# An encoder layer on one core: w_ga's weight units split by two DMAs from d = 2 on

## The chip, the cores and the metric

The kernel runs on one core of a Trainium2 chip. The metric is the device time of one execution in microseconds (us). A core has five engines that run their own instruction streams: PE (matrix products), DVE and ACT (elementwise work), POOL (elementwise work, and the issue of DMAs) and SP (here only the issue of DMAs). They wait for each other through semaphores, and each works strictly in the order of its stream. DMAs are issued on two queues here, SP's and POOL's; sixteen DMA engines carry out both.

## The reference

One layer of a bidirectional encoder, with 1024 positions and a model width of 1024, all in 32-bit floats. The part that the change touches is the merge of two branches:

```python
z = h @ w_in
u, v, q, k, va, gate_a, gate_b = jnp.split(z, cuts, axis=-1)
a_out = gmlp_branch(u, v, gm_v_g, gm_w_s, gm_b_s) @ w_a
b_out = window_attention_branch(q, k, va, q_norm_g, k_norm_g, attn_sink) @ w_b
merged = jax.nn.sigmoid(gate_a) * a_out + jax.nn.sigmoid(gate_b) * b_out
x = x + gt1 * (merged @ w_o)
```

`h` is the normalised and modulated input. A feed-forward sub-layer follows, which the change does not touch. The columns of `w_in` that give `gate_a` are called w_ga in the kernel, those for `gate_b` w_gb; w_a and w_b lie side by side in w_ab.

## The kernel before

**Products in three parts.** PE works on a 32-bit format with a shortened mantissa (`F32R`). To keep the accuracy, every operand is split into a high part, its value rounded to that format, and a low part, the rest. A product is then three: high by high, high by low, low by high, in this order (`mm3`, line 154).

**Units.** Weights come in units of 128 x 1024 values, 512 KB. `unit` (line 146) loads one over SP's queue into a tile called `raw`, lets ACT copy it into a tile `wh` (the copy rounds), and lets DVE subtract the two into a tile `wl`. The pool `wpool` has three buffers each for `raw`, `wh` and `wl`, so each new unit has to wait until the unit that holds its buffer is used up.

**Stages.** `half` (line 513) runs twice, each time over 512 of the positions: q, k and v, then attention mixed with the u products and the gates of d = 0 and 1, then a loop over d (line 868), then a loop for w_o (line 919). The feed-forward part follows. In the loop over d, tile d makes 128 of the 1024 output channels of `merged`, transposed. From d = 2 on it needs three units: w_gb[d], w_ab[d], w_ga[d]. PE's order in a tile is the w_gb gate (8 steps of 3 products of 128 x 128 by 128 x 512), the w_b product (4 steps of 3), the w_ga gate (8 steps of 3), the w_a product (4 steps of 3). ACT turns each gate's sum into a tanh, DVE multiplies it with the branch's product and adds the two, and the result is split for the w_o loop. Each tile also handles two (first half) or three (second half) units of w_ada2, which DVE reduces from `raw` tiles (`ada_next`, line 503); the first half loads a block of x as well.

**The order of the work.** From d = 2 on nothing fixes the order by hand: a scheduler orders each engine's stream, hands out the buffers and sets the waits. The units of the next tile are split while PE works on the present one. DMAs of SP's queue keep the order in which the program issues them (`load`, line 126). POOL issues the stores of x1 in the w_o loops and DMAs of the feed-forward part, and in the loop over d nothing from d = 2 on.

Of the kernel before, what the change touches and what calls it, by code (L numbers as in the profile page):

```python
# [8 lines left out]
F32 = mybir.dt.float32  # L9
F32R = mybir.dt.float32r  # L10
BF16 = mybir.dt.bfloat16
AF = mybir.ActivationFunctionType
ALU = mybir.AluOpType
# [3 lines left out]
P = 128  # L17
# [16 lines left out]
UNIT = 1024  # L34
# [4 lines left out]
def kernel(  # L39
# [22 lines left out]
    nc = tc.nc  # L62
# [19 lines left out]
    V, A, G, T = (Engine(e) for e in (nc.vector, nc.scalar, nc.gpsimd, nc.tensor))  # L82
# [4 lines left out]
    wpool = ctx.enter_context(pool("wpool", 3))  # L87
# [9 lines left out]
    def nm(s):  # L97
        n_names[0] += 1
        return f"{s}_{n_names[0]}"

    def mm_bank():
        return psum.tile([P, 512], F32, tag="mm", name=nm("mm"))
# [7 lines left out]
    def stream(tag):  # L110
        return t2.tile([P, 512], F32, tag=tag, name=nm(tag), bufs=2)

    def midt(dt, shape):
        return mid.tile([P, 2048], dt, tag="mid", name=nm("mid")).rearrange(
            "p (a b) -> p a b", a=shape
        )
# [9 lines left out]
    def load(dst, src):  # L126
        tc.keep_in_program_order(nc.sync.dma_start(dst, src))
# [13 lines left out]
    def raw_unit(src):  # L141
        r = wpool.tile([P, UNIT], F32, tag="raw", name=nm("raw"))
        load(r, src)
        return r

    def unit(src, eng=None, raw=None):
        r = raw if raw is not None else raw_unit(src)
        h = wpool.tile([P, UNIT], F32R, tag="wh", name=nm("wh"))
        l = wpool.tile([P, UNIT], F32R, tag="wl", name=nm("wl"))
        A.copy(h, r)  # L150
        (eng or V).tensor_tensor(l, r, h.bitcast(F32), op=ALU.subtract)
        return h, l

    def mm3(out, a, b, first, last):
        T.matmul(out, a[0], b[0], start=first, stop=False)
        T.matmul(out, a[0], b[1], start=False, stop=False)
        T.matmul(out, a[1], b[0], start=False, stop=last)
# [130 lines left out]
    def ss_tile():  # L288
        return small.tile([P, 640], F32, tag="ss", name=nm("ss"), bufs=1)
# [3 lines left out]
    def sumsq(src, first, ss):  # L293
        if first:
            A.activation(ss, src, AF.Square)
        else:
            q = tmp()
            A.activation(q, src, AF.Square)
            V.tensor_tensor(ss, ss, q, op=ALU.add)
# [10 lines left out]
    def split(src, dh, dl, eng=None):  # L310
        A.copy(dh, src)
        (eng or V).tensor_tensor(dl, src, dh.bitcast(F32), op=ALU.subtract)
# [190 lines left out]
    def ada_next(n):  # L503
        for _ in range(n):
            if ada_queue:
                col, gain = ada_queue.pop(0)
                ada_dot(raw_unit(w_ada2[col - GT1]), col)
                ada_end(col, gain)

    def x_rows(hf, k):  # L510
        return xT[k * P : (k + 1) * P, hf * HALF : (hf + 1) * HALF]

    def half(hf):
# [4 lines left out]
        if hf == 0:  # L518
# [33 lines left out]
            ada_dot(r[:, 1, :], SH1)  # L552
            V.reciprocal(rcol[0], root)
            wq = unit(None, V, wq0)
            wk = [wpool.tile([P, UNIT], F32R, tag=x, name=nm(x)) for x in ("wh", "wl")]
            A.copy(wk[0], wk0)
# [19 lines left out]
        for k in range(KT):  # L576
# [25 lines left out]
            if k == 4:  # L602
                wk = unit(w_kv[1], V)
            if k % 2 == 1 and k < KT - 1:
                wq_next = unit(w_q[(k + 1) // 2], V)
# [80 lines left out]
        def gate(wg):  # L686
            pg = mm_bank()
            gate_part(wg, pg, range(KT))
            return pg
# [161 lines left out]
        def gate_act(pg):  # L851
            sg = tmp()
            A.activation(sg, pg, AF.Tanh, scale=0.5)
            return sg
# [13 lines left out]
        for d in range(KT):  # L868
            if d % 4 == 0:
                mH[d // 4] = midt(F32R, 4)  # L870
                mL[d // 4] = midt(F32R, 4)
            ms = []
            in_order[0] = d < 2
            if d > 1:
                wg2 = unit(w_gb[d])
                wab = unit(w_ab[d])
                wg1 = unit(w_ga[d])
            else:
                wg1 = wg2 = None
                wab = units[9 + d]  # L880
            for (wg, o, br) in ((wg2, 512, (oH, oL)), (wg1, 0, (gH, gL))):
                sg = gate_act(gate(wg)) if d > 1 else sgs.pop(0)
                pb = mm_bank()
                for k in range(4):
                    kc = slice(o + k * P, o + (k + 1) * P)
                    mm3(pb, (wab[0][:, kc], wab[1][:, kc]),
                        (br[0][:, k, :], br[1][:, k, :]), k == 0, k == 3)
                V.scalar_tensor_tensor(out=sg, in0=sg, scalar=1.0, in1=pb, op0=ALU.add, op1=ALU.mult)
                ms.append(sg)
            V.tensor_tensor(ms[0], ms[0], ms[1], op=ALU.add)  # L890
            split(ms[0], mH[d // 4][:, d % 4, :], mL[d // 4][:, d % 4, :])
            in_order[0] = False
            if d > 1:
                ada_next(2 + hf)
            if hf == 0:
                xk = stream("hs")
                load(xk, x_rows(1, d))
                if d == 0:
                    ssn = ss_tile()[:, :HALF]
                in_order[0] = d == 0  # L900
                sumsq(xk, d == 0, ssn)
                in_order[0] = False
# [54 lines left out]
        sums.append(ss)  # L957

    half(0)
    half(1)  # L960


# [559 lines left out]
```

## Time and profile before

| what | value |
|---|---|
| time, median of 2 runs | 1256.95 us (1256.83 to 1257.07) |
| span of the profiled execution, first to last instruction | 1255.1 us |
| DMA packets | 67773, 214.25 MB |
| SP's queue | 155.59 MB |
| POOL's queue | 57.68 MB |
| read from HBM over the span | 170.24 MB |
| w_ga's loads | 16 of 512 KB on SP's queue, 4.0 us from issue to landing (median) |

The times are of the timed runs; the profile is of one execution, and its span leaves out what lies before the first and after the last instruction. In the profile's rows L75 is the line of a helper through which all engine calls go, so groups are told apart by the names of the tiles: out<-in, with shape, type, count, then busy time, the mean of one in ns, and the idle time of the engine before them with what ended it. PEld is the loading of weights into PE, which overlaps with the products. A row of the timeline has start and length in us, engine, line, operation and tiles. A row of the DMA issues has the queue, the count, the size and the median time in us from issue to landing.

### The profile page before, as it was taken

The page shows a single profiled execution, that of the slowest core. Times are in us where ns is not written, and L with a number is a line of the kernel's source. Part 1 is how long each engine was busy: PE and PEld are TensorE (multiplying, and loading weights), DVE is VectorE, ACT ScalarE, POOL GpSimd, SP SyncE. Part 2 cuts the span into 40 slices and gives each one's busy share as a digit, 9 for nine tenths or more (in the row PEclk, how much of TensorE's full clock was granted, in tenths as well). Part 3 has the DMA queues.
Part 4 walks back from the last instruction along what each step waited for, and adds up shares of the span by engine and source line. Part 5 has one row for each costly group of instructions (what it writes and reads, how often), then busy time and mean ns, then how long its engine had stood idle before and what let it go on. Part 6 is the DMA issues. An engine that isn't in the chain of part 4 may idle for free.

```text
span 1255.1 us, 15405 instructions
## 1 busy us (share of the span) xinstructions
PE 1234.1 (98%) x5714; PEld 1025.1 (82%) x5714; DVE 861.5 (69%) x1404; ACT 543.5 (43%) x867; POOL 132.7 (11%) x148
## 2 busy tenths in 40 slices
PE   5999999999999999999999999999999999999998
PEld 4888888888888888888888888888888887888887
DVE  8998875557468786666698766666666666455646
ACT  5467853334257772334454333333333334433342
POOL 0123310000032330000100000001010000010001
PEclk9999999999999999999999999999999999999999
DMA  9422145546522126665712454464554449896652
GB/s 362 169 84 67 52 143 184 177 159 211 197 70 67 51 89 196 201 194 209 250 36 102 147 189 151 154 213 182 205 189 180 168 168 357 280 328 187 196 161 101
DMA packets 67773, 214.25 MB, mean 171 GB/s; under 512 B 7793, under 2 KB 7793, under 8 KB 62450
## 3 DMA queue, kind: packets, MB, share of 16 engines
q1 hardware_dynamic: 56450, 155.59, 37.5%
q0 software_dynamic: 11248, 57.68, 12.7%
q8 instruction: 45, 0.74, 0.2%
q14 instruction: 30, 0.25, 0.1%
HBM read 170.24 MB, written 42.99 MB: 170 GB/s over the span
## 4 chain that ended last, share of the span: by engine, by line
PE 86%; DVE 6%; ACT 3%; DMA 3%; issue 1%; SPq 0%; POOL 0%; ACTq 0%; DVEq 0%
PE mm L75 47%; PE at L75 39%; DVE mid L75 2%; DVE wl L75 2%; ACT wh L75 1%; DMA mid<-in_w_ada_dram 1%; DMA hs<-in_xT_dram 1%; ACT lb L75 1%; DVE xs L75 0%; DMA mid<-in_xT_dram 0%; ACT mid L75 0%; DVE ws L75 0%; DMA raw<-in_w_o_dram 0%; DVE hid L75 0%; DMA raw<-in_w_q_dram 0%
## 5 line engine op out<-in xcount | busy, mean ns | idle before, releaser
L75 DVE TENSOR_TENSOR wl<-raw,wh 128x1024 fp32r<-128x1024 f32 x147 | 180.7, 1231 | 122.9 <-ACT wh L75 121.5
L75 ACT CAST wh<-raw 128x1024 fp32r<-128x1024 f32 x161 | 168.9, 1053 | 218.7 <-PE mm L75 126.7
L75 PE MATMUL mm<-mid,wh 128*128 128x512 f32 x736 | 227.8, 390 | 0.8 <-DVE mid L75 0.6
L75 PE MATMUL mm<-h,wh 128*128 128x512 f32 x608 | 187.9, 390 | 0.0
L75 PEld LDWEIGHTS mm<-mid,wh 128*128 128x128 f32 x736 | 137.7, 188 | 30.3 <-DVE mid L75 1.0
L75 PE MATMUL mm<-mid,wl 128*128 128x512 f32 x368 | 143.2, 389 | 0.0
L75 PEld LDWEIGHTS mm<-h,wh 128*128 128x128 f32 x608 | 113.7, 188 | 23.4
L75 PE MATMUL mm<-wh,h 128*128 128x512 f32 x384 | 129.7, 399 | 2.4 <-ACT h L75 2.3
L75 PE MATMUL mm<-h,wl 128*128 128x512 f32 x304 | 118.3, 389 | 0.0
L75 DVE TENSOR_TENSOR wl<-ws,wh 128x1024 fp32r<-128x1024 f32 (+1 forms) x55 | 62.0, 1128 | 43.6 <-ACT wh L75 43.6
L75 PEld LDWEIGHTS mm<-wh,h 128*128 128x128 f32 x384 | 71.7, 189 | 17.3 <-ACT h L75 3.2
L75 PEld LDWEIGHTS mm<-mid,wl 128*128 128x128 f32 x368 | 69.1, 188 | 14.4
L75 ACT CAST wh<-ws 128x1024 fp32r<-128x1024 f32 (+1 forms) x55 | 53.6, 974 | 58.6 <-DVE ws L75 42.1
L75 PE MATMUL mm<-wl,h 128*128 128x512 f32 x192 | 75.9, 395 | 0.0
L75 PE MATMUL at<-h,wh 128*128 128x512 f32 x240 | 74.1, 390 | 0.0
L75 PEld LDWEIGHTS mm<-h,wl 128*128 128x128 f32 x304 | 57.1, 188 | 12.0
L75 DVE SCALAR_TENSOR_TENSOR raw<-raw,silu_c 128x1024 f32<-128x1024 f32 x32 | 39.1, 1222 | 34.4 <-DMA raw<-in_w_ada_dram 33.5
L75 DVE TENSOR_TENSOR ol<-raw,oh 128x1024 fp32r<-128x1024 f32 x30 | 36.7, 1224 | 31.6 <-ACT oh L75 29.8
L75 ACT ACTIVATE xs<-xs 128x512 f32<-128x512 f32 x21 | 13.3, 633 | 96.4 <-DVE xs L75 96.4
L75 PE MATMUL at<-wl,wh 128*128 128x512 f32 x136 | 53.0, 390 | 0.7 <-DVE wl L75 0.7
L75 PE MATMUL at<-wh 128*128 128x512 f32 x136 | 53.0, 390 | 0.4 <-DVE mid L75 0.4
L75 PE MATMUL at<-wh,wl 128*128 128x512 f32 x136 | 52.9, 389 | 0.0
(244 smaller groups left out, 2459.8 us busy)
## 6 DMA issues: line engine op xcount, KB each, us to landing
raw<-in_w_ada_dram SPq DMA_DIRECT2D x32, 512.0 KB, 3.5
raw<-in_w_gate_dram SPq DMA_DIRECT2D x28, 512.0 KB, 4.1
tA<-hid POOLq DMA_DIRECT2D x11, 1024.0 KB, 5.0
tB<-hid POOLq DMA_DIRECT2D x11, 1024.0 KB, 4.9
wo<-in_w_out_dram POOLq DMA_DIRECT2D x22, 512.0 KB, 6.3
wS<-wo POOLq DMA_DIRECT2D x11, 1024.0 KB, 5.2
raw<-wS SPq DMA_DIRECT2D x44, 256.0 KB, 3.7
raw<-tB SPq DMA_DIRECT2D x44, 256.0 KB, 4.6
```

What stands on the lines that cost most here:

```text
L75: ins = f(*args, **kw)
```

## The change

From d = 2 on the units of w_ga are made by a new function. The high part is loaded straight from HBM into `wh` by a DMA on POOL's queue whose target type is `F32R`, so that it converts. ACT writes the negated high part into `wl`. A second DMA on POOL's queue then reads the same weights again and adds them onto what `wl` holds. No `raw` tile is used, and DVE has no part in it. w_gb's and w_ab's units, and w_ga's first two, are made as before.

```diff
+    def unit_by_dma(src):
+        h = wpool.tile([P, UNIT], F32R, tag="wh", name=nm("wh"))
+        l = wpool.tile([P, UNIT], F32R, tag="wl", name=nm("wl"))
+        nc.gpsimd.dma_start(h, src)
+        A.mul(l, h.bitcast(F32), -1.0)
+        nc.gpsimd.dma_start(l, src, accum_op=ALU.add)
+        return h, l
...
             if d > 1:
                 wg2 = unit(w_gb[d])
                 wab = unit(w_ab[d])
-                wg1 = unit(w_ga[d])
+                wg1 = unit_by_dma(w_ga[d])
```

## The prediction, made before the change was run

> **What bounds the kernel now.** I read the page's busy times first, then the table by stretches of time for the stages that the change touches, then the timeline of one tile in such a stage, then the DMA issues.
>
> ```profile
> span 1255.1 us, 15405 instructions
> ...
> PE 1234.1 (98%) x5714; PEld 1025.1 (82%) x5714; DVE 861.5 (69%) x1404; ACT 543.5 (43%) x867; POOL 132.7 (11%) x148
> ...
> L75 DVE TENSOR_TENSOR wl<-raw,wh 128x1024 fp32r<-128x1024 f32 x147 | 180.7, 1231 | 122.9 <-ACT wh L75 121.5
> L75 ACT CAST wh<-raw 128x1024 fp32r<-128x1024 f32 x161 | 168.9, 1053 | 218.7 <-PE mm L75 126.7
> ```
>
> PE is busy in all but 1255.1 - 1234.1 = 21.0 us. That is a ceiling for any gain: with every idle moment of PE gone, the time falls by 21.0 of 1257, 1.7%. The last two rows are the two halves of today's split of a weight unit: the cast to the high part, 1.053 us on ACT, and the subtraction for the low part, 1.231 us on DVE.
>
> ```profile
> core 0: us, PE busy (x) PEld busy (x) DVE busy (x) ACT busy (x) POOL busy (x), PEclk, DMA share, GB/s
> 168.80:279.00 110.20, 110.20 (x491) 91.15 (x490) 65.40 (x98) 37.13 (x50) 1.16 (x1) 1.00 0.54 174
> 279.00:327.00 48.00, 47.92 (x219) 39.57 (x218) 35.23 (x49) 19.01 (x25) 5.91 (x9) 1.00 0.72 245
> 464.00:577.00 113.00, 112.67 (x501) 93.45 (x502) 71.51 (x112) 34.15 (x42) 0.00 (x0) 1.00 0.59 191
> 577.00:627.00 50.00, 50.00 (x230) 41.62 (x229) 35.62 (x47) 22.38 (x29) 5.42 (x9) 1.00 0.70 247
> ```
>
> The first and third rows are the loops over d in which w_ga is used, one for each half of the positions; the second and fourth are the w_o loops behind them. In all four PE has no idle time worth naming (0.41 us together). DVE is idle in 40% of the first stretch and ACT in 66%. So work taken off DVE or ACT here brings PE nothing; only a new wait of PE can move the time, and it moves it in full.
>
> Now one tile, d = 3 of the first half, in the timeline:
>
> ```profile
> 195.66 0.39 PE L75 MATMUL mm<-mid,wl 128*128 128x512 f32 x1
> 195.89 0.61 PE L75 MATMUL mm<-h,wh 128*128 128x512 f32 x2
> ...
> 204.05 0.61 PE L75 MATMUL mm<-h,wh 128*128 128x512 f32 x2
> ```
>
> A tile is four groups on PE: the w_gb gate (24 products), the w_b half of w_ab (12), the w_ga gate (24), the w_a half of w_ab (12). It starts at 195.89, and w_ga's first product is at 204.05: 36 products in 8.16 us, 0.227 us each. A whole tile is 72 x 0.227 = 16.3 us.
>
> **What the change does to that tile.** Removed for each of 12 tiles (d = 2 to 7, both halves): one load on SP's queue, one cast (1.053 us, ACT), one subtraction (1.231 us, DVE). Added: two DMAs on POOL's queue and one negation on ACT. DVE gives back 12 x 1.231 = 14.8 us, ACT trades a cast for an instruction of the same size (taken at 1.05 us); neither is waited for by PE, so their worth is nothing, and no stall of today goes.
>
> What matters is when the new chain can start. In the order that the scheduler writes for the changed kernel, w_ga's new high tile takes the buffer that w_ab's held in the tile before (three buffers of each kind, three units a tile, these two trade places every tile), and the converting DMA therefore waits for the last w_a product of the tile before, that is for the tile's start. The old path has the same release, but a short way behind it:
>
> ```profile
> 184.22 0.33 SPq L127 DMA_DIRECT2D raw<-in_w_ga_dram  x1
> ...
> 195.48 0.33 SPq L127 DMA_DIRECT2D raw<-in_w_gb_dram  x1
> 195.86 1.06 ACT L75 CAST wh<-raw 128x1024 fp32r<-128x1024 f32 x1 [0.66 <-PE mm L75]
> ...
> 197.72 1.22 DVE L75 TENSOR_TENSOR wl<-raw,wh 128x1024 fp32r<-128x1024 f32 x1
> ...
> 279.14 1.39 POOL L75 TENSOR_TENSOR rcol<-ms,nhalf 128x4 f32<-128x4 f32 x1 [109.19 <-DVE ms L75]
> ```
>
> Today the weights are fetched at 184.22 into a raw tile of their own, 11 us before the buffer comes free; behind the release are only the cast at 195.86 and the subtraction, over at 198.94, 5.1 us before PE asks. In the changed kernel both trips to HBM lie behind the release, one after the other, since the second adds onto what the negation wrote. POOL itself is free (109 us idle), so the first issue goes out about 0.2 us after the release, as ACT's cast does today (195.66 to 195.86).
>
> No row shows a converting or an adding DMA. The rows that bound them:
>
> ```profile
> wo<-in_w_out_dram POOLq DMA_DIRECT2D x22, 512.0 KB, 6.3
> wS<-wo POOLq DMA_DIRECT2D x11, 1024.0 KB, 5.2
> ...
> raw<-in_w_gb_dram SPq DMA_DIRECT2D x16, 512.0 KB, 3.5
> ...
> mid<-x1d POOLq DMA_DIRECT2D x4, 1024.0 KB, 12.5
> ```
>
> and, for everything that writes or reads the tile wo on POOL's queue, the spread:
>
> ```profile
> DMA to landing us min/median/max: 3.8/5.3/8.2
> ```
>
> Converting DMA: 512 KB on POOL's queue like the wo loads, so 3.8 to 8.2 us. I take the median, 5.3, not the minimum, since SP sends the loads of w_gb (195.48) and w_ab into the same moment. Adding DMA: it moves the same 512 KB and must also read the 512 KB that it adds to. At best it is a plain load, 3.8; at worst the slowest 1024 KB row, 12.5. I take 6.3, the nearest row over the 5.2 of a 1024 KB store.
>
> Chain from the release to the low part: 0.2 + 5.3 + 0.1 + 1.05 + 0.1 + 6.3 + 0.1 = 13.15 us (0.1 us estimated for each hand-over). Cover: the 36 products, 8.16, and w_ga's first two, which need the high part alone, 0.45: 8.61 us. Left over as a stall of PE: 4.5 us a tile. The period becomes 16.3 + 4.5, since the next release waits for the tile's end: the stall repeats and is not paid once. 12 x 4.5 = 54 us.
>
> Who else waits. On ACT the negation stands ahead of the cast of w_gb for the next tile and the tanh of this tile's w_gb gate; it ends at 0.2 + 5.3 + 0.1 + 1.05 = 6.7 us, and the w_gb gate ends at 5.4 us, so both start 1.3 us late. What needs them (DVE's product with the w_b sum, the next tile's w_gb gate) is due after 8.2 us and after the stall: hidden, 1.3 us a tile if the stall were not there. On POOL's queue the second DMA waits for ACT, with nothing behind it but the next tile's DMA, which waits for a later event anyway; in the first half the power for the row sums (279.14) follows long after. SP loses an issue and gains no wait. In the w_o loops behind, nothing is moved.
>
> A second cost comes with the stall, since a PE that has rested does not run at full rate:
>
> ```profile
> 23.36 0.63 PE L75 MATMUL mm<-wl,h 128*128 128x512 f32 x1
> ...
> 25.92 0.63 PE L75 MATMUL mm<-wl,h 128*128 128x512 f32 x1
> ...
> 29.36 0.39 PE L75 MATMUL mm<-wl,h 128*128 128x512 f32 x1
> ...
> 30.27 0.39 PE L75 MATMUL mm<-wl,h 128*128 128x512 f32 x1
> ```
>
> After the kernel's idle start the products come every (25.92 - 23.36) / 6 = 0.43 us, and a little later every (30.27 - 29.36) / 4 = 0.23 us. Eight came at the slow rate, 8 x 0.2 = 1.6 us lost. Whether a rest of 4.5 us is enough for that, no row tells: it costs 0 to 1.6 us a tile, and I take half, 0.8; 12 x 0.8 = 10 us. [...]
>
> Sum: 54 + 10 = 64 us on the profiled 1255.1, so a span of 1319. The two timed runs have their median at 1256.95, 1.85 over that span; carried over, the forecast is **1321 us**, 5.1% slower.
>
> **Rivals.** *The chain fits.* Place: between the tile's start and w_ga's third product. If both DMAs went like SP's w_gb loads, 3.5 us, the chain would be 0.2 + 3.5 + 0.1 + 1.05 + 0.1 + 3.5 + 0.1 = 8.55, under the cover of 8.61, and the time stays at 1257. It decides as long as the two landings together take 7.05 us or less. For it: POOL's queue is empty here, and the w_gb loads run at 3.5 in this very stage. Against it: POOL's best is 3.8, two of which already leave 0.5 us a tile (1264 us with no clock loss), and both DMAs do more than copy. [...]
>
> *The DMAs are far slower than copies.* If converting and adding are done at a fraction of the copy rate, 8.2 and 12.5 us, the chain is 22.25 and the stall 13.6 us; with 1.6 for the clock every time, 12 x 15.2 = 183 us, 1440. For it: no row shows either operation. Against it: the amounts are small, and the 12.5 us row shares the queues with other stores.
>
> *Faster.* DVE's 14.8 us and the raw tiles no longer used by w_ga could let other loads start earlier. The place where that could show is PE's idle time, 21.0 us in all, of which 0.4 lies in the four stretches above; the best case is some tenths of a microsecond.
>
> **How the numbers follow.** A measurement of this kernel can tell about 2%, 25.1 us, from no change: 2.1 us a tile. The forecast (over 2.1 us a tile, up to about 11) gets 0.70. The fitting chain and its neighbours up to 2.1 us get 0.17: they need both landings at 9.1 us together or less. Far slower DMAs get 0.12. Faster by over 2% would need more than PE's whole idle time: 0.01. So slower by over 2% has 0.82. The range runs from two plain POOL loads at their best, 1264, to a stall of 11 us a tile, 1257 + 132 = 1389; it leaves out the fully fitting chain (0.07) and the slow tail.
>
> **What would show it.** In the changed profile: PE idle before w_ga's products for some 50 us, ended by the DMA into wl, with 12 waits of 3 to 6 us; PE's busy time within 15 us of 1234; two rows of 12 DMAs on POOL's queue, landing at about 5.3 and 6.3 us; an ACT row of 12 negations near 1.05 us; DVE down by 15 us; the first loop over d taking 110 + 6 x 5.3 = 142 us. Matmuls of the group after each wait at 0.43 us apart would show the clock. The forecast is wrong if the two landings come under 9 us together, if the first DMA leaves before the tile's start, or if PE waits on something other than the low part.

## The result, and the profile after

The changed kernel takes 1333.29 us, the median of 2 runs (1329.93 and 1336.65), against 1256.95: a ratio of 1.0605 (95% interval 1.0542 to 1.0669). The profiled execution has a span of 1328.2 us, 73.1 over the 1255.1 of before. The page after, its lines that answer to those of before and the two largest groups of PE that use w_ga's tiles:

```profile
span 1328.2 us, 15426 instructions
...
PE 1263.7 (95%) x5714; PEld 1042.8 (79%) x5714; DVE 850.1 (64%) x1392; ACT 542.2 (41%) x867; POOL 149.7 (11%) x172
...
L75 PE MATMUL mm<-h,wh 128*128 128x512 f32 x608 | 205.9, 422 | 0.0
L75 PE MATMUL mm<-h,wl 128*128 128x512 f32 x304 | 130.8, 430 | 44.1 <-DMA wl<-in_w_ga_dram 44.1
```

The same two groups before:

```profile
L75 PE MATMUL mm<-h,wh 128*128 128x512 f32 x608 | 187.9, 390 | 0.0
L75 PE MATMUL mm<-h,wl 128*128 128x512 f32 x304 | 118.3, 389 | 0.0
```

PE makes the same 5714 products, and both its columns have grown: its busy time by 1263.7 - 1234.1 = 29.6 us, and, in the last row of the first block, 44.1 us of idle time that the DMA into `wl` ends. Before, the two groups had means of 390 and 389 ns and no idle time. 29.6 + 44.1 = 73.7 us is the growth of the span within a microsecond. DVE has 11.4 us less to do and PE gains nothing by it.

The table of PE's waits gives total, number and longest; the DMA issues give count, size and median time from issue to landing:

```profile
PE mm L75 <- DMA wl<-in_w_ga_dram: 44.1, 12, 7.4
```

```profile
wh<-in_w_ga_dram POOLq DMA_DIRECT2D x12, 512.0 KB, 4.5
wl<-in_w_ga_dram POOLq DMA_DIRECT2D x12, 512.0 KB, 5.6
```

One wait in each of the twelve tiles, 3.7 us in the mean. The timeline of tile d = 3 of the first half, the one that was shown of before:

```profile
200.61 0.62 PE L75 MATMUL mm<-h,wh 128*128 128x512 f32 x2
200.85 0.55 POOL L157 DMA_DIRECT2D wh<-in_w_ga_dram  x1 [14.32 <-PE mm L75]
...
205.46 1.06 ACT L75 ACTIVATE wl<-wh 128x1024 fp32r<-128x1024 f32 x1 [2.59 <-DMA wh<-in_w_ga_dram]
...
206.82 0.88 POOL L159 DMA_DIRECT2D wl<-in_w_ga_dram  x1 [5.42 <-ACT wl L75]
...
208.77 0.61 PE L75 MATMUL mm<-h,wh 128*128 128x512 f32 x2
...
212.38 0.79 PE L75 MATMUL mm<-h,wl 128*128 128x512 f32 x1 [2.99 <-DMA wl<-in_w_ga_dram]
...
217.66 0.63 PE L75 MATMUL mm<-h,wl 128*128 128x512 f32 x1
218.09 0.72 PE L75 MATMUL mm<-h,wh 128*128 128x512 f32 x2
```

Read it from the top. The tile starts at 200.61; POOL has been waiting 14.32 us for PE and sends the converting DMA 0.24 us later. ACT has been idle when the high part lands (205.46), negates in 1.06 us, and POOL sends the adding DMA at 206.82, 0.30 us behind ACT. PE is through with the 36 products and with w_ga's first two, and from there on has nothing until 212.38. The whole chain is 212.38 - 200.61 = 11.77 us; less the cover of 8.61 that is 3.16 us of stall. From 212.38 to 218.09 PE makes 13 products, one every 0.44 us; behind them comes the usual pace. Thirteen times 0.21 us is another 2.8 us. Together 6 us are added to a tile of 16.3.

The stall returns at an even distance. The first and the sixth wait of the first half:

```profile
191.32 0.79 PE L75 MATMUL mm<-h,wl 128*128 128x512 f32 x1 [3.46 <-DMA wl<-in_w_ga_dram]
...
301.46 0.79 PE L75 MATMUL mm<-h,wl 128*128 128x512 f32 x1 [4.07 <-DMA wl<-in_w_ga_dram]
```

Five tiles in 110.14 us are 22.0 us a tile against 16.3.

What the slow products are is seen when the stretch around the wait is cut into windows of 3.41 us. Columns: from:to, length, PE busy (products), granted clock, share of the DMA engines, GB/s (a packet counts in the window in which it starts, so that the share can pass 1):

```profile
204.65:208.06 3.41, 3.41 (x16) 1.00 0.54 179
208.06:211.47 3.41, 1.32 (x6) 1.00 1.05 201
211.47:214.88 3.41, 2.50 (x6) 0.50 0.81 317
214.88:218.30 3.42, 3.42 (x9) 0.50 0.01 2
218.30:221.71 3.41, 3.41 (x16) 1.00 0.00 0
```

The granted clock falls to half at 211.47, while PE still rests, and returns at 218.30. The half clock lasts for 6.83 us, although the wait was 2.99 us. All twelve waits are followed by such a stretch: six of 3.41 us, five of 6.83, one of 10.24.

### The profile page after: what moved, and what is told of

It reads as the page before. It is cut to its first block, busy times and chain, and to the rows that moved or that the text cites. A ratio compares the mean times of both kernels' runs of the same rounds, so it can differ in the third digit from the quotient of the medians.

```text
span 1328.2 us, 15426 instructions
## 1 busy us (share of the span) xinstructions
PE 1263.7 (95%) x5714; PEld 1042.8 (79%) x5714; DVE 850.1 (64%) x1392; ACT 542.2 (41%) x867; POOL 149.7 (11%) x172
## 4 chain that ended last, share of the span: by engine, by line
PE 67%; issue 16%; DVE 7%; DMA 5%; ACT 3%; POOL 1%; SPq 0%; POOLq 0%; ACTq 0%; DVEq 0%
PE at L75 35%; PE mm L75 33%; DVE wl L75 2%; DVE mid L75 2%; DMA wl<-in_w_ga_dram 1%; ACT wh L75 1%; DMA wh<-in_w_ga_dram 1%; DMA raw<-in_w_ada_dram 1%; DMA mid<-in_w_ada_dram 1%; DVE ws L75 1%; DVE hid L75 1%; DMA wo<-in_w_out_dram 1%; ACT lb L75 1%; DVE xs L75 1%; DMA wS<-wo 0%
## 5 line engine op out<-in xcount | busy, mean ns | idle before, releaser
L75 DVE TENSOR_TENSOR wl<-raw,wh 128x1024 fp32r<-128x1024 f32 x135 | 166.1, 1232 | 210.3 <-ACT wh L75 210.2
L75 ACT CAST wh<-raw 128x1024 fp32r<-128x1024 f32 x149 | 156.0, 1051 | 261.7 <-issue 131.9
L75 PE MATMUL mm<-h,wh 128*128 128x512 f32 x608 | 205.9, 422 | 0.0
L75 PE MATMUL mm<-h,wl 128*128 128x512 f32 x304 | 130.8, 430 | 44.1 <-DMA wl<-in_w_ga_dram 44.1
L75 PEld LDWEIGHTS mm<-h,wh 128*128 128x128 f32 x608 | 126.1, 208 | 28.1
L75 PEld LDWEIGHTS mm<-h,wl 128*128 128x128 f32 x304 | 63.5, 209 | 63.0 <-DMA wl<-in_w_ga_dram 49.1
L75 ACT ACTIVATE xs<-xs 128x512 f32<-128x512 f32 x21 | 13.3, 632 | 96.8 <-DVE xs L75 96.8
```

Of the source, the lines that this page charges most:

```text
L75: ins = f(*args, **kw)
```

## The experiments

The question was whether the loss is what the prediction said (a chain longer than its cover, with the clock behind it), or whether the two DMAs harm by their traffic or are slow for reasons of their own. Ten kernels were timed, the last of the table twice and the others four times each. The kernel before, timed beside them, was between 1256.57 and 1256.77 in the median.

| kernel | time, us | ratio (95%) | PE's wait for the DMA into wl: us, times |
|---|---|---|---|
| high part alone by DMA | 1265.48 | 1.0073 (1.0056 to 1.0089) | none |
| low part alone by DMA | 1313.47 | 1.0444 (1.0416 to 1.0472) | 29.6, 12 |
| w_ga ahead of w_ab | 1280.52 | 1.0209 (1.0182 to 1.0236) | 16.6, 11 |
| low part used last | 1281.92 | 1.0199 (1.0160 to 1.0237) | 14.2, 7 |
| these two together | 1265.13 | 1.0075 (1.0058 to 1.0092) | 0.2 |
| w_ga ahead of both others | 1273.11 | 1.0126 (1.0111 to 1.0142) | none |
| 14 more products in the gap | 1316.19 | 1.0472 (1.0450 to 1.0495) | 14.6, 8 |
| second DMA does not add | 1304.44 | 1.0363 (1.0331 to 1.0395) | 31.2, 12 |
| one more load beside it | 1355.62 | 1.0785 (1.0767 to 1.0803) | 72.9, 12 |
| plain DMA, not waited for | 1270.0 | 1.0107 (1.0087 to 1.0127) | none |

### One DMA of the two

The high part alone by DMA, with the low part made by DVE from a raw tile as before:

```diff
     def unit_by_dma(src):
+        r = raw_unit(src)
...
         nc.gpsimd.dma_start(h, src)
-        A.mul(l, h.bitcast(F32), -1.0)
-        nc.gpsimd.dma_start(l, src, accum_op=ALU.add)
+        V.tensor_tensor(l, r, h.bitcast(F32), op=ALU.subtract)
```

> Keeps the converting DMA for the high part, and makes the low part as before: DVE subtracts the high part from a raw tile that SP's queue has loaded early. Theory of the chain (two trips to HBM in a row behind the release of the buffer, with 8.6 us of cover): one trip is left, 0.2 + 4.5 + 0.1 + 1.2 + 0.1 = 6.1 us behind the release, under the 8.2 us until the high part is wanted, so no stall and no slow clock: 1257 us, at most 1260. Rival (DMAs of this kind on POOL's queue slow the stage through the shared DMA engines, wherever they stand): one of the two is still there, so about half of the loss stays, 1290 to 1300 us.

1265.48 us: most of the loss is gone with the second trip to HBM, and the time is far under the 1290 to 1300 of the rival. It is still 5 us above the 1260 that was the most expected. What is left is a new wait, in the second half only:

```profile
PE mm L75 <- DVE wl L75: 7.4, 4, 4.0
```

The longest of the four in DVE's timeline:

```profile
529.55 1.23 DVE L75 SCALAR_TENSOR_TENSOR raw<-raw,silu_c 128x1024 f32<-128x1024 f32 x1 [3.88 <-DMA raw<-in_w_ada_dram]
...
533.40 1.22 DVE L75 SCALAR_TENSOR_TENSOR raw<-raw,silu_c 128x1024 f32<-128x1024 f32 x1
...
534.55 1.22 DVE L75 TENSOR_TENSOR wl<-raw,wh 128x1024 fp32r<-128x1024 f32 x1
...
535.82 0.79 PE L75 MATMUL mm<-h,wl 128*128 128x512 f32 x1 [4.02 <-DVE wl L75]
```

The subtraction at 534.55, which PE resumes on at 535.82, stands in DVE's stream behind reductions of w_ada2, the first of which waited 3.88 us for its load. That is read from the rows and was not tested.

The low part alone by DMA, with load, cast and high part as before:

```diff
     def unit_by_dma(src):
+        r = raw_unit(src)
...
-        nc.gpsimd.dma_start(h, src)
+        A.copy(h, r)
         A.mul(l, h.bitcast(F32), -1.0)
         nc.gpsimd.dma_start(l, src, accum_op=ALU.add)
```

> Keeps the negation and the adding DMA, and makes the high part as before by a cast on ACT from a raw tile loaded early. Theory of the chain: 0.2 + 1.05 + 1.05 + 0.1 + 5.6 + 0.1 = 8.1 us behind the release against a cover of 8.6, so it fits by 0.5 us: 1257 us, up to 1265 where the adding DMA lands late in some tiles. Rival (the adding DMA is the trouble by itself): most of the loss stays, over 1300 us.

1313.47 us: a miss, by 48 us. One DMA behind the buffer's release should have fitted under the cover, with the landing of 5.6 us. It did not land in 5.6:

```profile
wl<-in_w_ga_dram POOLq DMA_DIRECT2D x12, 512.0 KB, 8.5
```

The timeline of the moment in which it leaves, SP's and POOL's issues:

```profile
198.82 0.33 SPq L127 DMA_DIRECT2D raw<-in_w_gb_dram  x1
...
200.19 0.33 SPq L127 DMA_DIRECT2D raw<-in_w_ab_dram  x1
...
200.57 0.42 SPq L127 DMA_DIRECT2D raw<-in_w_ga_dram  x1
...
201.57 0.90 POOL L160 DMA_DIRECT2D wl<-in_w_ga_dram  x1 [18.81 <-DVE mod L75]
```

Three loads of 512 KB go out on SP's queue in the 2.8 us ahead of it. The chain is not a sum of fixed landings: taking the first DMA away moved the second into the company of SP's loads. That these loads make the landing longer is what the rows suggest; the kernel with one more load, further down, bears on it.

### More cover

w_ga's unit asked for ahead of w_ab's, so that it takes the buffers that w_ga's own last unit leaves, 12 products ahead of the tile's end:

```diff
                 wg2 = unit(w_gb[d])
-                wab = unit(w_ab[d])
                 wg1 = unit_by_dma(w_ga[d])
+                wab = unit(w_ab[d])
```

> The changed kernel with the unit of w_ga asked for before that of w_ab, so that it takes the buffer that w_ga's own unit held in the tile before, which comes free 12 products (2.7 us) earlier; both DMAs and the negation stay. Theory of the chain: cover 8.6 + 2.7 = 11.3 us, chain 0.2 + 4.5 + 0.1 + 1.05 + 0.1 + 5.6 + 0.1 = 11.65 us, a stall of 0.3 us a tile, too short for the clock: 1257 + 4 = 1261 us, at most 1275. Rival (contention, or the DMAs by themselves): unchanged at 1330 us.

The eight products of w_ga's gate with the low part put behind the sixteen with the high part:

```diff
+            for k in range(KT):
+                kc = slice(k * P, (k + 1) * P)
+                T.matmul(pg, wg[0][:, kc], hH[k // 4][:, k % 4, :], start=k == 0, stop=False)
+                T.matmul(pg, wg[0][:, kc], hL[k // 4][:, k % 4, :], start=False, stop=False)
+            for k in range(KT):
+                kc = slice(k * P, (k + 1) * P)
+                T.matmul(pg, wg[1][:, kc], hH[k // 4][:, k % 4, :], start=False, stop=k == KT - 1)
```

> The changed kernel with the products of w_ga's gate in another order: all 16 that need the high part first, the 8 with the low part last; nothing else is moved. Theory of the chain: the low part is wanted 14 products (3.2 us) later, cover 8.6 + 3.2 = 11.8 us against 11.65: no stall of more than some tenths, no slow clock, 1257 to 1262 us. Rival (PE waits for something other than the low part, the high part or a bank): the wait moves and stays, over 1300 us.

1280.52 and 1281.92 us. Either edit takes 52 us off the changed kernel and leaves more than was expected, 5 us above the upper figure of the first and 20 above that of the second. In the first the adding DMA lands later than it did, 6.9 us against 5.6; in the second seven waits remain, the longest 6.3 us in the first tile. So cover was short, and the landings are not the same from kernel to kernel. Both edits together:

> Two earlier edits of the changed kernel together: w_ga's unit is asked for ahead of w_ab's, and the eight products of w_ga's gate with the low part come last. Theory (the chain against its cover): the start moves 12 products ahead, 2.7 us, and the low part is wanted 14 products later, 3.2 us, so the cover is 8.6 + 2.7 + 3.2 = 14.5 us. With the landings that the first of these edits alone had, the chain is 0.2 + 4.8 + 0.1 + 1.05 + 0.1 + 6.9 + 0.1 = 13.25 us, so no wait for the DMA into wl is left but for the first tile of a half (up to 3.6 us), and the time is 1257 to 1268 us. Rival (the landings grow with every edit that moves them into other loads, so that what is gained in cover is lost in landing): waits of 10 us or more stay, and the time is 1272 us or more.

1265.13 us. The group that had the waits:

```profile
L75 PE MATMUL mm<-h,wl 128*128 128x512 f32 x304 | 104.8, 390 | 0.2 <-DMA wl<-in_w_ga_dram 0.2
```

0.2 us instead of 44.1 and a mean of 390 ns, though the landings are the longest of the four, 5.3 and 6.9 us in the median. With 14.5 us of cover the chain fits. Both DMAs still move the same bytes, and the time is 68 us below the changed kernel's: so much of the loss was the short cover and the clock behind it. The 8 us that are left over the kernel before are not explained by it (7.2 us in the profile: 2.9 of PE's busy time and 4.3 of waits for other things). (The row's busy time is below the 118.3 of before because a record of 0.39 us overlaps the next one, 0.227 us later, and a row counts the overlap of neighbours of its own kind once; PE's sum is 1237.0.)

The whole unit earlier still, ahead of w_gb's, with nothing else changed:

```diff
+                wg1 = unit_by_dma(w_ga[d])
                 wg2 = unit(w_gb[d])
                 wab = unit(w_ab[d])
-                wg1 = unit_by_dma(w_ga[d])
```

> The changed kernel with w_ga's unit asked for first in each tile (w_ga, w_gb, w_ab), so that its tiles take the buffers that w_gb's units leave after 24 of a tile's 72 products, and w_gb's take those that w_ga's leave 12 products ahead of the tile's end. The two DMAs, the negation and all products are the same. Theory (the chain from the buffer's release to the low part is longer than the products that cover it, and nothing else is wrong): the chain may start 48 products, 48 x 0.227 = 10.9 us, earlier; cover 8.6 + 10.9 = 19.5 us against a chain of 12 to 14 us, so PE's waits for the DMA into wl go, the clock drops go with them, and the time is 1257 to 1265 us. w_gb's cast and subtraction then have 12 products, 2.7 us, for 2.5 us of work, so up to 1 us a tile may show there (1269). Rival (the second reading of w_ga and the converting writes slow PE or the other loads by themselves, wherever they start): 1300 us or more with PE's products still at 0.42 us or more in the mean.

1273.11 us, 8 above the expected 1257 to 1265 and 4 above the 1269 that allowed for the new order. No wait for either of the two DMAs is left, and PE's products with `h` and `wh` are at 395 ns, near the 390 of before: the second reading of w_ga and the adding do not slow PE's products by themselves. What is left is a wait for DVE, named in the expectation but larger than it said:

```profile
PE mm L75 <- DVE wl L75: 12.6, 5, 3.4
```

```profile
491.36 1.23 DVE L75 SCALAR_TENSOR_TENSOR raw<-raw,silu_c 128x1024 f32<-128x1024 f32 x1 [4.69 <-DMA raw<-in_w_ada_dram]
...
492.81 1.23 DVE L75 TENSOR_TENSOR wl<-raw,wh 128x1024 fp32r<-128x1024 f32 x1
...
494.09 0.50 PE L75 MATMUL mm<-h,wl 128*128 128x512 f32 x1 [3.08 <-DVE wl L75]
```

w_gb's subtraction has little time now, and in the second half it again stands behind a reduction that waits for a load of w_ada2. These waits of DVE for w_ada2's loads have grown; the first row is of the kernel before, the second of this one:

```profile
DVE raw L75 <- DMA raw<-in_w_ada_dram: 33.5, 17, 4.0
DVE raw L75 <- DMA raw<-in_w_ada_dram: 88.7, 29, 4.7
```

With the high part alone by DMA they are 60.9 us, with both edits 82.8. So the change may also cost something through w_ada2's loads, whose median landing here is 4.2 us against 3.5 before. Whether the two DMAs delay these loads, or the raw tiles that now go round in another order, was not tested. It concerns the 8 to 16 us that are left in these three kernels, not the other 60 and more.

### The clock

Fourteen products that nobody reads, of w_ga's first high part, in the gap:

```diff
+            T.matmul(pg, wg[0][:, :P], hH[0][:, 0, :], start=True, stop=False)
+            T.matmul(pg, wg[0][:, :P], hL[0][:, 0, :], start=False, stop=False)
+            idle = at_bank()
+            for _ in range(14):
+                T.matmul(idle, wg[0][:, :P], hH[0][:, 0, :], start=True, stop=True)
+            T.matmul(pg, wg[1][:, :P], hH[0][:, 0, :], start=False, stop=False)
```

> The changed kernel with 14 further products of w_ga's high part, written to a bank of their own that nobody reads, between w_ga's first two products and its first product with the low part. They take 14 x 0.227 = 3.2 us, which is most of the wait of 3.7 us a tile, so that PE is busy in it. Theory (PE's slower products, 29.6 us in all, come only from the rest before them): no slow stretch is left behind the wait, the clock stays at full rate, and the time is 1257 + 12 x 3.2 to 3.9 = 1295 to 1305 us, faster than the changed kernel by some 30 us although PE does 168 products more. Rival (the products are slow because of the traffic of the two DMAs, not because of the rest): the slow products stay, and the time is 1330 us or more.

1316.19 us: 168 products more and 17 us less than the changed kernel. PE and its wait in this profile:

```profile
PE 1281.2 (97%) x5882; PEld 1059.4 (80%) x5882; DVE 850.5 (65%) x1392; ACT 542.0 (41%) x867; POOL 149.8 (11%) x172
```

```profile
PE mm L75 <- DMA wl<-in_w_ga_dram: 14.6, 8, 5.2
```

Of the 47.1 us that PE is busier than before, 168 x 0.227 = 38.1 are the new products, so 9.0 us are left for products at less than the full rate, against 29.6. The clock falls after three waits instead of twelve, those of 2.8, 4.3 and 5.2 us. Where PE worked through the gap, its products behind it were at full rate, beside the same DMAs: the slow products come from the rest of PE and not from the traffic. The time was 11 us above the expected range because the wait that is left is 14.6 us, more than the few microseconds that the subtraction of means (3.7 - 3.2 a tile) had given; the waits differ too much from tile to tile for it.

### What the DMAs cost

The second DMA without adding, so that the low part is the high part once more:

```diff
-        nc.gpsimd.dma_start(l, src, accum_op=ALU.add)
+        nc.gpsimd.dma_start(l, src)
```

> The changed kernel with the second DMA writing instead of adding: it replaces what the negation wrote, so that w_ga's low part is a second high part and its output is not the reference's; the waits and the bytes read from HBM stay. Theory (adding costs the difference between the two rows of DMA issues, 5.6 against 4.5 us): the second DMA lands in 4.5 us like the first, its issue on POOL takes 0.55 us and not 0.87, the wait falls from 3.7 to about 2.6 us a tile, 31 us in all, and the time is 1300 to 1320 us. Rival (it is slower because of what else is in flight, not because it adds): it still lands in 5.4 to 5.7 us and the time is 1325 to 1337 us.

1304.44 us, as the first theory said. Its landings:

```profile
wh<-in_w_ga_dram POOLq DMA_DIRECT2D x12, 512.0 KB, 4.7
wl<-in_w_ga_dram POOLq DMA_DIRECT2D x12, 512.0 KB, 4.4
```

4.4 us without and 5.6 with adding: adding 512 KB costs 1.2 us here. A landing is counted from the start of the issue, and POOL's issue of the adding DMA is longer as well, 0.88 us against the 0.54 of the one that only writes (d = 3), so some 0.3 us of the 1.2 lie on POOL. PE's wait fell from 44.1 to 31.2 us, 1.1 a tile.

One more load of SP, started when the negation is done, into a raw tile that is not read:

```diff
         A.mul(l, h.bitcast(F32), -1.0)
+        r = wpool.tile([P, UNIT], F32, tag="raw", name=nm("raw"))
+        A.mul(r[:, :1], l[:, :1].bitcast(F32), 1.0)
+        load(r, src)
         nc.gpsimd.dma_start(l, src, accum_op=ALU.add)
```

> The changed kernel with one more load of 512 KB in each of the 12 tiles, on SP's queue into a raw tile that nobody uses, made to start when the negation is done, so in the same moment as the adding DMA. Theory (the adding DMA shares the sixteen DMA engines with what is in flight, which is why it took 8.5 and not 5.6 us beside three loads of SP in the kernel that fetched only the low part by DMA): it lands about 1 us later, at 6.4 to 7.0 us, PE's wait grows by as much to some 4.7 us a tile, and the time is 1340 to 1352 us. Rival (loads of the other queue do not matter): it lands in 5.4 to 5.8 us as before, and the time is 1328 to 1338 us.

1355.62 us, a little over the expected range, with a landing not of 6.4 to 7.0 us but of 9.0. The landing and the timeline of SP and POOL around it:

```profile
wl<-in_w_ga_dram POOLq DMA_DIRECT2D x12, 512.0 KB, 9.0
```

```profile
209.38 0.33 SPq L127 DMA_DIRECT2D raw<-in_w_ga_dram  x1
...
209.66 0.88 POOL L162 DMA_DIRECT2D wl<-in_w_ga_dram  x1 [4.88 <-ACT raw L75]
209.80 0.86 SPq L127 DMA_DIRECT2D raw<-in_w_ada_dram  x2
210.71 0.42 SPq L127 DMA_DIRECT2D hs<-in_xT_dram  x1
```

The load did more than was meant: it held up SP's queue until the negation was done, so that w_ada2's two loads and the block of x leave within 1.4 us behind it. The adding DMA thus went out beside three loads of 512 KB, as in the kernel that fetched only the low part, and the two agree: 9.0 and 8.5 us, some 3 us over the 5.6, which is about 1 us for each load, an estimate. The 5.6 is no landing without neighbours either: in the changed kernel two of SP's loads leave while the adding DMA is under way (208.75 and 209.89 us in d = 3). No run separates the number of loads from the moment in which they leave.

A plain DMA in place of the adding one, into a raw tile that is not read; the low part is the negated high part alone:

```diff
         A.mul(l, h.bitcast(F32), -1.0)
-        nc.gpsimd.dma_start(l, src, accum_op=ALU.add)
+        r = wpool.tile([P, UNIT], F32, tag="raw", name=nm("raw"))
+        A.mul(r[:, :1], l[:, :1].bitcast(F32), 1.0)
+        nc.gpsimd.dma_start(r, src)
```

> The changed kernel with a plain DMA on POOL's queue in place of the adding one: it starts in the same moment, reads the same 512 KB and writes them unconverted into a raw tile that nobody reads. The low part is the negated high part alone, so the output is not the reference's. It measures what converting costs, and what one DMA alone in the chain costs. Theory: the chain is 0.2 + 4.5 + 0.1 + 1.05 = 5.9 us under a cover of 8.6, so PE waits for nothing, its products are at full rate, and the time is 1257 to 1264 us. If converting costs time as adding does (1.2 us), the plain DMA lands in 3.2 to 3.8 us; if it does not, in 4.2 to 4.8 us like the converting one in its place.

1270.0 us, 6 above the expected range, with no wait for the DMA in the chain. (What is left of PE's waits is for DVE and ACT, and behind one of them, of 2.8 us, the clock drops once; which buffer or load causes it was not followed up.) The landing of the plain DMA:

```profile
raw<-in_w_ga_dram POOLq DMA_DIRECT2D x12, 512.0 KB, 3.8
```

Plain 3.8, converting 4.4, adding 5.6 us, each for 512 KB sent right behind the negation: converting costs some 0.6 us and adding 1.2 more. The 0.6 is the weaker figure, since raw tiles and with them SP's loads were shifted in that kernel.

No variant beat the kernel before; with 21.0 us of idle PE time in all of it, there was little to win.

## Why the prediction was right

Forecast 1321 us in a range of 1264 to 1389, slower at 0.82; measured 1333.29. The mechanism was right in each of its steps; two sizes were off, in opposite directions, the wait 10 us too long and the clock 20 us too short. That the sum comes so near is luck in part.

| step | forecast | measured |
|---|---|---|
| release to the first issue | 0.2 us | 0.24 (d = 3) |
| converting DMA | 5.3 (3.8 to 8.2) | 4.5 median |
| hand-over, negation, hand-over | 1.25 | 1.36 from ACT's start (d = 3: 1.06 and 0.30) |
| adding DMA | 6.3 (3.8 to 12.5) | 5.6 median |
| stall, twelve tiles | 54 | 44.1 |
| slow products, twelve tiles | 10 | 29.6 |
| sum | 64 | 73.1 (span) |

**Where the chain starts.** At the tile's start, by the release of the last w_a product: in the timeline POOL waits 14.32 us for PE and issues 0.24 us behind it. Moving that start ahead by 12 products, or by 48, took the wait down to 16.6 us and to nothing.

**The landings.** Both bounds held; the values taken were 0.8 and 0.7 us too long. For the converting DMA the wo rows were the nearest ones and yet slower than this stage. The 5.3 was not even theirs: it is the median of the wo loads and the 1024 KB stores of wo together, and the loads alone have 6.3, as the first of the four rows says. With 6.3 the forecast would have been 12 us longer and nearer to the measured time, by a landing that is further from the measured 4.5. The sum of the two, 10.1 us, is over the 9 us below which the forecast was to be wrong. The experiments show that a landing is no property of the operation alone: the adding DMA took from 5.6 to 9.0 us with the loads beside it.

**The period.** That the stall repeats in each tile and is not paid once: twelve waits, 22.0 us from tile to tile against a forecast of 16.3 + 5.3 = 21.6. The first loop over d took 144.2 us, from its first product (168.10) to the row sums behind it (312.25), against 109.3 before (168.58 to 277.84) and a forecast of 142. One wait, 7.4 us in the second half's first tile, lies above the 3 to 6 us that were named, and three, of 2.5 to 3.0, just below.

**The clock: the mis-sized term.** The forecast said 0 to 1.6 us a tile, "and I take half, 0.8". Measured are 2.5 us. Two things were wrong with the bound. It came from eight slow products at the kernel's start, 8 x 0.43 = 3.4 us; here six of the twelve stretches at half clock are longer, five of 6.83 us and one of 10.24, as the rows around 211.47 show for one of the five. And the half was for the doubt whether so short a rest is enough: it was in all twelve tiles, with waits of 2.54 to 7.41 us.

**What hides at nothing.** DVE's group of subtractions shrank by 180.7 - 166.1 = 14.6 us as forecast, and PE's other waits are those of before. PE's busy time was to stay within 15 us of 1234; it did not, by the clock.

**The rivals.** *The chain fits*: no, 10.1 us of landings against the 7.05 that it needed; by cover instead of by speed it does fit, in the kernel with both edits. The 3.5 us of SP's w_gb loads, which the rival took for both DMAs, were not reached on POOL's queue: the plain DMA took 3.8 us and the two kinds of this change 4.5 and 5.6. *Far slower*: no, 4.5 and 5.6 against 8.2 and 12.5. *Faster*: no.

## What to carry to other kernels

A tile that is filled in place by a converting and an adding DMA has both trips to HBM behind the release of its buffer (in d = 3 the first left 0.24 us behind it), where the load into a tile of its own left some 11 us ahead of it. Before such a change, count the work that lies between the release and the first use, and compare it with the sum of the landings as they are among the other loads of that stage; if it is short, ask for the unit earlier or use the low part last. And price such a stall of PE above its length: 44.1 us of waiting cost 73.1 here, 1.7 times as much. In the other kernels with such waits (the one with 14 more products aside) it was 1.3 to 1.7 times: 1.3 where the waits were about 6 us each (72.9 us cost 96.8), and 1.4 where they were about 1.5 us (16.6 us cost 22.6). The factor belongs to this kernel and is not a rule.

## What the runs showed of the hardware that was not expected

**The clock was at half after a wait of 1.83 us, but not after each longer one.** In the profile of the changed kernel the granted clock changes at 190.99, 194.40, 211.47, 218.30 and 235.36 us, which are 1, 5, 2 and 5 times 3.413 us apart, while the rests of PE before the changes to half begin at 187.86, 209.38 and 231.75. The shortest of the twelve waits, 2.54 us, has 3.41 us at half clock behind it. Two shorter waits, in the kernel without adding, each with the 3.41 us that follow (columns as above; the ends of products are modelled in the profile, so the lengths of rests are by its account):

```profile
231.05:234.46 3.41, 1.58 (x7) 1.00 0.90 297
234.46:237.87 3.41, 3.41 (x10) 0.50 0.34 139
271.99:275.41 3.42, 1.67 (x8) 1.00 0.89 270
275.41:278.82 3.41, 3.41 (x16) 1.00 0.38 153
```

Behind the 1.83 us of rest the next 3.41 us are at half clock and hold 10 products; behind the 1.75 us they are at full clock and hold 16. The length of the rest does not decide it alone: behind 2.60 us in the kernel with w_ga ahead of w_ab (582.15 to 584.75) and 3.08 us in the one with w_ga ahead of both others (the wait that ends at 494.09) the products come every 0.23 us. What else decides it is not shown. The two runs of the changed kernel are 0.5% apart where those of before are 0.02% apart; whether the clock is the reason was not tested.

**Beside three loads the adding DMA landed about 3 us later.** Adding 512 KB cost 1.2 us (5.6 against 4.4) and converting some 0.6 (4.4 against 3.8); with three loads of 512 KB that leave in the 3 us around it the adding DMA took 8.5 and 9.0 us against 5.6. The last is read from two kernels that agree and was not taken apart further.
